# Two-layer diffusion backbone on one core: where the convolution and pooling steps, the prompt's pooling, the first early pairs and two stores stand in the order of work

## The chip, the core and the metric

The kernel runs on one core of one Trainium2 chip. The metric is the device time of one execution in microseconds (us); three runs are shown as their median. The profile is of one execution of its own.

## What is computed

Two layers over 1024 sample tokens and 128 prompt tokens, width 1024, in float32. Cut to what matters:

```python
def trunk_layer(x, cond, ...):
    mod = silu(cond) @ w_mod + b_mod                 # shift, scale, gate
    hn = rms_norm(x, g_pre) * (1 + scale) + shift
    a_b, a_c, a_x, a_z, q_down, kv_down, b_z, c_u, c_z, merge_logits = split(hn @ w_in)
    y_a = silu(a_z) * (a_b * centred_conv3(a_c * a_x, conv_w, conv_b))
    y_b = silu(b_z) * attention(q_down, kv_down, cached latents, rope)
    y_c = silu(c_z) * multiscale_pool(c_u, pool_w, pool_scale)   # windows 2, 4, 8, 16
    gates = sigmoid(merge_logits)
    merged = sum over n of gates[n] * ([y_a, y_b, y_c][n] @ w_branch[n])
    return x + gate * rms_norm(merged @ w_o, g_post)
```

The sample pass and the prompt pass share the weights. `multiscale_pool` takes, for each of four groups of 128 channels, the mean over a window along the tokens, subtracts the input, and multiplies by a 128 by 128 matrix.

## The kernel before

Every float32 operand of a product is split into a high part, rounded for TensorE, and the rest, and a product is three matmuls (high by high, low by high, high by low; `mm3`, line 109). ScalarE or GpSimd makes the high part (`a_copy` line 67, `p_copy` line 82), VectorE the rest (`sub`, line 90). The tokens stand in two chunks of 512 columns. SBUF has 44 slots `S` of 1040 columns and 12 slots `H` of 512, PSUM 8 banks `PS`. Each engine executes its instructions in the order in which the Python program emits them, and so do the DMA queues of SP, ScalarE and GpSimd; so the order of emission is the schedule.

A layer has these stages.

- **Input product** (`in_phase`, line 829). The columns of `w_in` are taken as 29 pairs of 256 columns. Each pair (class `Pair`, line 562) has a generator `prep` (line 567): it asks SP for the raw weights, then makes splits, one piece for each call. Twenty pairs are *full*, in the order of `ORDER` (line 822): 8 to 15, 19 to 22, 16, 17, 18, 23, 24, 26, 27, 28. A full pair (`run`, line 688) makes seven products of 12 matmuls each (a Strassen form over halves of the weights and both chunks) and one product for the prompt. Nine pairs (`EARLY`, line 27) are cut in two: two products of the first chunk and the prompt's product are done *early* (line 656), while the second chunk is still being normalised, and the other five products *late*, after all full pairs. The early stage takes the first three pairs together, in loops over products, and the others singly.
- **What a pair leaves** is stored to DRAM: gates, the convolution's factors (pairs 8 to 15, two for each of four blocks of channels: `d_t` and `d_zb`), the latents (16 to 18), the pooling's inputs and gates (19 to 22, one for each group: `d_u`, `d_z`).
- **Background generators.** `spawn` (line 135) puts a generator on a list, and each `tick` (line 139) calls every one of them once; a full pair makes four ticks, a late one three. `conv_gen` (line 870) does the convolution of the sample tokens, six calls for each of four blocks, and goes on with `s_pool` (line 1017), four groups with windows 2, 4, 8 and 16. A group loads its input, adds shifted copies of it (`window_sum`, line 981: one, two, three or four additions of some 1030 columns, in one call), makes means, splits, multiplies, and stores `d_yc`. It is spawned after pair 15. `p_conv` (line 898) does the prompt's convolution and goes on with the prompt's pooling (`p_pool`, line 1055, 15 calls); it is spawned after pair 28, the last full pair. `mod_bg` (line 339) makes the modulation rows of later use, in layer 0.
- **Stores that wait.** `put` (line 118) emits a store on SP three `step`s later, so that SP doesn't stand before data that is not there yet; `flush` emits all of them at once. A store emitted with `sp.dma_start` directly makes SP wait for its data, and all later loads with it.
- **Merges** (`mid_phase`, line 1214). `merge` (line 932) multiplies a branch by its weights and gates and adds; the first takes the convolution's output, the second the pooling's. Each makes 26 ticks. During the first, `kv_lat` normalises and turns the key latents; during the second run `p_kv` (line 1165, the prompt's latents, with two transposes on TensorE, each three pauses after the row norm that it needs) and `q_lat` (query latents, with a column sum of squares on TensorE, a product with a matrix of ones).
- **Attention** (`produce`, `attention`), the third merge (`last_merge`), and the **output product** (`out_phase`, line 1775): `post_chunk` (line 1711) normalises a chunk, adds the residual and, in layer 0, makes the next layer's input and its early form; `out_prompt` (line 1758) does the same for the prompt. Between the layers, the splits of the first two early pairs of layer 1 are made during the last output group (`ahead`, line 633), and the rest of both chunks' norms is on the background list while the early pairs run.

## Time and profile before

| | us |
|---|---|
| median of 3 runs | 2816.55 |
| lowest and highest | 2812.87 and 2819.08 |
| the profiled execution's own time | 2811.16 |
| its span, first to last instruction | 2809.4 |

The profile is that one execution. A busy TensorE is not TensorE at its peak, and the granted clock of TensorE has two levels, 2.4 GHz (written 1.00) and 1.2 GHz (0.50); the mean over a stretch is given. In the order of time a row is a run of like instructions of one engine, with its start, its length, their count, and in brackets how long the engine had stood idle before it and what ended that. A row of the busy time by stage gives the stretch and its length, then busy time and count of instructions of PE, PEld, DVE, ACT and POOL, then the granted clock, the share of DMA and GB/s.

### The profile page before, as it was taken

What the parts mean: (1) busy time and instruction counts of PE and PEld (TensorE: products, weight loads), DVE (VectorE), ACT (ScalarE), POOL (GpSimd) and SP (SyncE); (2) the same over time, 40 slices, a digit from 0 to 9 for tenths busy, and PEclk for the clock granted to TensorE, in tenths of its full rate; (3) what the DMA queues carried; (4) which work ended last, traced back from release to release, by engine and by line L of the source; (5) the groups of instructions that cost most, each with busy time, mean ns of one, the idle gap of its engine ahead of it and who ended that gap; (6) DMA issues with size and microseconds to landing.
All of it is one profiled execution on the core that took longest, in us unless ns stands there. A gap on an engine that the chain in (4) does not pass through costs nothing. (4 is left out here: it accounts for less than half of the span.)

```text
span 2809.4 us, 32642 instructions
## 1 busy us (share of the span) xinstructions
PE 2578.5 (92%) x11672; PEld 2040.9 (73%) x11672; DVE 1836.5 (65%) x2434; ACT 1024.5 (36%) x1694; POOL 893.1 (32%) x757
## 2 busy tenths in 40 slices
PE   4899999997898889999978999999979988999997
PEld 2777777775676767777757888887857766776786
DVE  5745566676656578886567565766767557888655
ACT  4521122232221357773344222223223124677621
POOL 2222211112122545753022232111222145477502
PEclk7999999998999999999989999999989999999999
DMA  7333245555479300006154222443535871000333
GB/s 280 126 115 108 94 162 178 189 171 168 136 270 323 131 5 8 23 31 201 57 180 155 95 71 83 163 160 130 185 126 191 283 265 27 5 8 31 120 117 113
DMA packets 218403, 371.02 MB, mean 132 GB/s; under 512 B 21120, under 2 KB 106112, under 8 KB 218240
## 3 DMA queue, kind: packets, MB, share of 16 engines
q1 hardware_dynamic: 186560, 308.36, 33.1%
q10 hardware_dynamic: 27072, 43.79, 4.2%
q0 software_dynamic: 4608, 16.78, 1.7%
q8 instruction: 92, 1.51, 0.2%
q14 instruction: 71, 0.58, 0.1%
HBM read 254.45 MB, written 112.23 MB: 131 GB/s over the span
## 5 line engine op out<-in xcount | busy, mean ns | idle before, releaser
L107 PE MATMUL p<-s,s 128*128 128x512 f32 (+3 forms) x10876 | 2459.2, 385 | 132.4 <-ACT s L68 40.7
L107 PEld LDWEIGHTS p<-s,s 128*128 128x128 f32 (+1 forms) x10876 | 1945.2, 190 | 618.4 <-ACT s L68 49.3
L88 DVE TENSOR_TENSOR s<-s,s 128x1024 fp32r<-128x1024 f32 (+7 forms) x565 | 662.3, 1180 | 381.3 <-ACT s L68 155.0
L88 POOL TENSOR_TENSOR s<-s,s 128x512 f32<-128x512 f32 (+2 forms) x109 | 203.7, 1872 | 764.2 <-DMA s<-in_w_in_dram 605.5
L88 DVE TENSOR_TENSOR h<-p,h 128x512 f32<-128x512 f32 (+1 forms) x480 | 315.2, 659 | 197.4 <-PE p L107 125.8
L68 ACT CAST s<-s 128x1024 fp32r<-128x1024 f32 (+4 forms) x283 | 276.9, 988 | 452.1 <-DVE s L88 273.7
L88 DVE TENSOR_TENSOR s<-h,s 128x512 fp32r<-128x512 f32 (+4 forms) x316 | 298.4, 956 | 118.6 <-ACT s L79 60.8
L82 POOL TENSOR_SCALAR s<-s 128x1024 fp32r<-128x1024 f32 (+2 forms) x123 | 149.4, 1217 | 496.4 <-DVE s L88 123.8
L79 ACT ACTIVATE h<-h 128x512 f32<-128x512 f32 (+1 forms) x196 | 123.2, 629 | 470.7 <-DVE h L88 354.4
L79 ACT ACTIVATE h<-p 128x512 f32<-128x512 f32 (+2 forms) x364 | 208.5, 573 | 229.1 <-PE p L107 214.0
L79 ACT ACTIVATE s<-p 128x512 fp32r<-128x512 f32 x288 | 174.1, 604 | 2.4 <-POOL h L88 2.4
L88 DVE TENSOR_TENSOR h<-h,h 128x512 f32<-128x512 f32 (+3 forms) x122 | 89.7, 735 | 119.8 <-ACT h L79 95.2
L88 POOL TENSOR_TENSOR s<-s 128x512 f32<-128x512 f32 x94 | 131.9, 1414 | 77.7 <-DVE s L88 45.1
L1492 DVE TENSOR_REDUCE c<-p 128x1 f32<-128x448 f32 x256 | 147.8, 610 | 5.5 <-PE p L107 5.4
L68 ACT COPY h<-p 128x512 f32<-128x512 f32 (+2 forms) x108 | 51.6, 478 | 235.1 <-PE p L107 219.7
L88 POOL TENSOR_TENSOR h<-h,h 128x512 f32<-128x512 f32 (+2 forms) x72 | 96.3, 1338 | 105.5 <-DVE h L88 68.2
L88 POOL TENSOR_TENSOR s<-h,s 128x512 fp32r<-128x512 f32 x64 | 89.7, 1402 | 115.9 <-ACT s L79 113.3
L88 DVE TENSOR_TENSOR s<-p,s 128x512 f32<-128x512 f32 (+2 forms) x118 | 71.4, 631 | 51.6 <-PE p L107 21.5
L68 ACT CAST s<-h 128x512 fp32r<-128x512 f32 (+5 forms) x92 | 47.8, 524 | 152.8 <-DVE h L88 91.5
L68 ACT COPY s<-p 64x512 f32<-64x512 f32 (+3 forms) x116 | 64.1, 567 | 98.7 <-PE p L107 70.2
L88 POOL TENSOR_TENSOR s<-s,h 128x512 f32<-128x512 f32 x26 | 39.9, 1542 | 116.8 <-DVE h L100 76.3
L103 POOL TENSOR_SCALAR s<-s,cols 128x512 f32<-128x512 f32 x24 | 29.8, 1252 | 97.6 <-ACT s L79 68.3
(116 smaller groups left out, 933.1 us busy)
## 6 DMA issues: line engine op xcount, KB each, us to landing
s<-in_w_in_dram SPq DMA_DIRECT2D x296, 256.0 KB, 4.6
s<-in_w_mod_dram SPq DMA_DIRECT2D x48, 512.0 KB, 5.8
d_gate<-h ACTq DMA_DIRECT2D x96, 256.0 KB, 3.3
s<-d_gate SPq DMA_DIRECT2D x64, 256.0 KB, 5.7
d_part<-s SPq DMA_DIRECT2D x64, 256.0 KB, 2.2
s<-in_w_br_dram SPq DMA_DIRECT2D x24, 512.0 KB, 3.8
s<-in_xT_dram SPq DMA_DIRECT2D x16, 512.0 KB, 7.6
d_ya<-s SPq DMA_DIRECT2D x16, 512.0 KB, 2.6
```

What stands on the lines that cost most here:

```text
L68: act.copy(out=out, in_=in_)
L79: act.activation(out=out, in_=in_, func=func, scale=scale, bias=bias)
L82: pool.tensor_scalar(out=out, in0=in_, scalar1=1.0, scalar2=0.0, op0=ALU.mult, op1=ALU.add)
L88: eng.tensor_tensor(out=out, in0=in0, in1=in1, op=op)
L103: (eng or dve).tensor_scalar(out=out, in0=in0, scalar1=s1, scalar2=s2, op0=op0, op1=op1)
L107: pe.matmul(out=out, lhsT=lhsT, rhs=rhs, start=start, stop=stop)
L1492: dve.reduce_max(out=mv[:, i, qt:qt + 1], in_=ps[:, 0:448], axis=AX.X)
```

## The change

- `conv_gen` is spawned after pair 8. A list `done` holds the number of the last full pair that is through (never going down until the next layer's pair 8). Block m of the convolution waits until pair 9 + 2m is through, group gi of the pooling until pair 19 + gi; until then a call does nothing.
- `window_sum` becomes the generator `window_gen`, which pauses after each addition; `s_pool` passes the pauses on, `pooled` (the prompt) doesn't.
- `p_pool` is no longer the end of `p_conv`; it is spawned at the start of `mid_phase`, with its output slot, and has to be finished when the first merge is.
- In `early`, the first three pairs are made ready one by one, each just before its first product, and no longer all three before the first.
- In `p_kv` each of the two groups of three pauses becomes seven.
- The stores of `d_x` use `put`; the store of `d_xp` goes to GpSimd's queue. `post_chunk` pauses after its loads for the second chunk too.
- In `out_phase` of layer 0 the calls of `post_chunk` and `out_prompt` that followed the last prompt product are put into a generator `first`, which the early stage of layer 1 calls once, after the first early product.

```diff
@@ early
             first, steps = len(us) > 1, 2 if us[0] in units[-2:] else 1
+            p1 = []
             for u in us:
                 ready(u)
-            p1 = []
-            for u in us:
                 h = H()
                 a_copy(h, u.prod(u.w[0], 0, "11"))
@@ in_phase
             run(l, x, epis[x.p], None if last else u[i + 1], hooks)
-            if x.p == 15:
+            if x.kind == "full":
+                done[0] = max(x.p, done[0])
+            if x.p == 8:
+                done[0] = 8
                 g1 = spawn(conv_gen(l))
-            elif x.p == 24:
-                g1_done = g1
             if x.p == 28:
-                ypc.append(S(F32R))
-                g2 = spawn(p_conv(l, yp, ypc[0]))
+                g2 = spawn(p_conv(l, yp))
         finish(g2)
-        return ya, yp, ypc[0]
+        return ya, yp
@@ conv_gen
-        flush()
         for m in range(4):
+            while done[0] < 9 + 2 * m:
+                yield
+            flush()
             t, v = S(), S()
...
-        flush()
         yield from s_pool(l)
@@ p_conv
-        yield from p_pool(l, ypc)
@@ window_sum, now window_gen
             d = o
-        return d, tiles[(gi + 1) % 2]
+            yield
+        got += [d, tiles[(gi + 1) % 2]]
@@ s_pool
         for gi in range(4):
+            while done[0] < 19 + gi:
+                yield
+            flush()
             u = S()
...
-            d, o = window_sum(u, gi, 1024, [S(), S()])
-            yield
-            means(d, o, u, gi, 1024)
+            got = []
+            yield from window_gen(u, gi, 1024, [S(), S()], got)
+            o = got[1]
+            means(got[0], o, u, gi, 1024)
             yield
@@ p_kv, in both places
-            yield
-            yield
-            yield
+            for _ in range(7):
+                yield
@@ mid_phase
-        yc = []
+        yc, ypc = [], S(F32R)
+        gp = spawn(p_pool(l, ypc))
...
-        finish(R["first"])
+        finish(R["first"], gp)
@@ post_chunk
         xs = load_x(l, c)
-        if not quick:
-            yield
+        yield
...
-            sp.dma_start(out=d_x[c, kp], in_=outs[i][:, 0:1024])
+            put(d_x[c, kp], outs[i][:, 0:1024])
@@ out_prompt
-            sp.dma_start(out=d_xp, in_=out[:, 0:1024])
+            pool.dma_start(out=d_xp, in_=out[:, 0:1024])
@@ out_phase
-        gB = spawn(post_chunk(l, 1, B, True))
+        gB = post_chunk(l, 1, B, True)
+        next(gB)
+        gP = out_prompt(l, xp, gps, out, cs)
         if l + 1 < L:
-            prompt(0, lambda: next(gB, None))
-        else:
-            prompt(1, lambda: adv(gB, 2))
-            next(gB)
             prompt(0)
-        if l + 1 < L:
-            next(gB)
-        gP = out_prompt(l, xp, gps, out, cs)
+
+            def first():
+                for g in (gB, gB, gP, gB, gP, gB):
+                    next(g)
+                spawn(gB), spawn(gP)
+                yield
+
+            return (gP, gB), units, first()
+        prompt(1, lambda: adv(gB, 2))
+        next(gB)
+        prompt(0)
         next(gP, None)
         next(gB, None)
-        if l + 1 < L:
-            next(gP)
-            next(gB)
-        spawn(gP)
-        return (gP, gB), units if l + 1 < L else None
+        return (gP, gB), None, None
@@ the loop over layers
-            R = mid_phase(l, *in_phase(l, units, None if l else mid(), pend))
+            R = mid_phase(l, *in_phase(l, units, then if l else mid(), pend))
...
-            pend, units = out_phase(l, mg, pt)
+            pend, units, then = out_phase(l, mg, pt)
```

## Rows read from the trace of the kernel before

**Rows 1.** The page: busy time of TensorE, and its slices.
```profile
PE 2578.5 (92%) x11672; PEld 2040.9 (73%) x11672; DVE 1836.5 (65%) x2434; ACT 1024.5 (36%) x1694; POOL 893.1 (32%) x757
...
PE   4899999997898889999978999999979988999997
```

**Rows 2.** Busy time by stage: full and late pairs, layer 0, then layer 1.
```profile
397.00:640.00 243.00, 241.27 (x1154) 187.38 (x1153) 155.72 (x188) 65.36 (x89) 37.59 (x36) 1.00 0.50 168
640.00:818.00 178.00, 150.35 (x629) 116.22 (x627) 123.49 (x192) 41.66 (x68) 41.35 (x45) 0.91 0.54 181
...
1741.00:2012.40 271.40, 266.82 (x1286) 220.92 (x1285) 184.86 (x206) 74.96 (x101) 47.04 (x42) 1.00 0.44 149
2012.40:2176.10 163.70, 143.74 (x589) 113.77 (x587) 113.69 (x179) 41.27 (x67) 42.32 (x45) 0.93 0.52 171
```

**Rows 3.** Order of time, late pairs of layer 0.
```profile
673.36 7.65 DVE L88 TENSOR_TENSOR s<-s 128x1039 f32<-128x1039 f32 x4
...
681.67 0.69 PE L908 MATMUL p<-ident,s 128*128 128x128 f32 x2 [6.73 <-DVE h L88]
...
689.60 8.50 PE L107 MATMUL p<-s,s 128*128 128x512 f32 x24 [7.24 <-DVE h L100]
...
728.86 1.30 POOL L88 TENSOR_TENSOR s<-s,s 128x512 f32<-128x512 f32 x1 [24.66 <-DMA s<-in_w_in_dram]
...
743.31 1.87 PE L107 MATMUL p<-sel,h 128*128 128x2 f32 x8 [11.22 <-ACT h L68]
```

**Rows 4.** Order of time, late pairs of layer 1.
```profile
2042.32 6.85 DVE L88 TENSOR_TENSOR s<-s 128x1039 f32<-128x1039 f32 x4
...
2049.92 4.90 PE L107 MATMUL p<-s,s 128*128 128x512 f32 x12 [6.38 <-DVE h L88]
...
2075.73 14.05 PE L107 MATMUL p<-s,s 128*128 128x512 f32 x60
...
2105.91 14.20 PE L107 MATMUL p<-s,s 128*128 128x512 f32 x48 [4.58 <-DVE h L88]
```

**Rows 5.** VectorE by line and shape, 397 to 640 us: busy, mean ns, idle before.
```profile
L88 DVE TENSOR_TENSOR s<-s,s 128x1024 fp32r<-128x1024 f32 x44 | 55.3, 1257 | 36.6 <-ACT s L68 26.2 <-PE p L107 10.2
...
L88 DVE TENSOR_TENSOR s<-s 128x1039 f32<-128x1039 f32 x3 | 3.7, 1234 | 0.0
```

**Rows 6.** Order of time, start of the second merge of layer 0.
```profile
885.35 4.48 SPq L1130 DMA_DIRECT2D s<-d_kvq  x6
...
892.87 0.90 PE L1182 MATMUL p<-ident,h 128*128 128x128 f32 x3 [8.18 <-DVE h L103]
...
894.45 2.58 DVE L88 TENSOR_TENSOR s<-s,s 128x1024 f32<-128x1024 f32 x2 [1.63 <-ACT s L79]
...
899.28 1.88 PE L107 MATMUL p<-s,ones 128*128 128x512 f32 x4
```

**Rows 7.** Order of time, the prompt's pooling in layer 0: two calls.
```profile
777.10 0.98 DVE L88 TENSOR_TENSOR s<-s 128x143 f32<-128x143 f32 x3
...
779.48 0.29 DVE L88 TENSOR_TENSOR s<-s,s 128x128 fp32r<-128x128 f32 x1 [0.41 <-ACT s L68]
...
789.98 1.31 DVE L88 TENSOR_TENSOR s<-s 128x143 f32<-128x143 f32 x4
...
792.65 0.29 DVE L88 TENSOR_TENSOR s<-s,s 128x128 fp32r<-128x128 f32 x1 [0.36 <-ACT s L68]
```

**Rows 8.** Order of time, between the layers.
```profile
1438.95 1.45 PE L107 MATMUL p<-h,ones 128*128 128x512 f32 x2 [4.02 <-DVE h L88]
...
1457.25 0.44 ACT L79 ACTIVATE c<-c 128x1 f32<-128x1 f32 x2 [1.36 <-POOL c L103]
...
1460.73 0.80 PE L107 MATMUL p<-s,s 128*128 128x512 f32 x1 [12.84 <-ACT s L68]
...
1480.00 1.48 PE L107 MATMUL p<-h,ones 128*128 128x512 f32 x2 [3.37 <-DVE h L88]
```

**Rows 9.** Order of time, the first early pairs of layer 0.
```profile
60.56 1.22 PE L107 MATMUL p<-s,s 128*128 128x512 f32 x2 [10.77 <-ACT s L79]
```

More of the change, by code (lines that the diff above doesn't have):

```diff
@@ L837, in in_phase @@
         flush()
-        ya, yp, ypc = [], S(F32R), []
+        ya, yp = [], S(F32R)
         def load_ya(m):
@@ L894, in conv_gen, with p_conv @@
             yield
-        flush()
         yield from s_pool(l)
-    def p_conv(l, yp, ypc):
+    def p_conv(l, yp):
         tz = S()
@@ L979, in merge, with window_gen @@
         flush()
-    def window_sum(u, gi, n, tiles):
+    def window_gen(u, gi, n, tiles, got):
         w = n + 16
@@ L985, in window_sum @@
         s = 1
-        for step in range(gi + 1):
-            o = tiles[step % 2]
-            if step == 0:
+        for step_ in range(gi + 1):
+            o = tiles[step_ % 2]
+            if step_ == 0:
                 lo += 1
@@ L995, in window_sum @@
             d = o
-        return d, tiles[(gi + 1) % 2]
+            yield
+        got += [d, tiles[(gi + 1) % 2]]
     def pooled(u, gi, n, tiles):
-        d, o = window_sum(u, gi, n, tiles)
-        means(d, o, u, gi, n)
-        return o
+        got = []
+        for _ in window_gen(u, gi, n, tiles, got):
+            pass
+        means(got[0], got[1], u, gi, n)
+        return got[1]
     def means(d, o, u, gi, n):
@@ L1015, in hybrid_step_kernel @@
     PW = {}
+    done = [0]
     def s_pool(l):
@@ L1030, in s_pool @@
                 split(pw[0], pw[1], raw)
-            d, o = window_sum(u, gi, 1024, [S(), S()])
-            yield
-            means(d, o, u, gi, 1024)
+            got = []
+            yield from window_gen(u, gi, 1024, [S(), S()], got)
+            o = got[1]
+            means(got[0], o, u, gi, 1024)
             yield
@@ L1195, in p_kv @@
             ts(eq[:, 0:384], eq[:, 0:384], r, 0.0)
-            yield
-            yield
-            yield
+            for _ in range(7):
+                yield
             pt = PS()
@@ L1212, in kvq_post, with mid_phase @@
         return R
-    def mid_phase(l, ya, ypa, ypc):
+    def mid_phase(l, ya, ypa):
         lead[0] = 4
@@ L1713, in post_chunk @@
         xs = load_x(l, c)
-        if not quick:
-            yield
+        yield
         r = rstd(bsum(O_["acc"]), DM)
@@ L1805, in out_phase @@
         finish(gA)
-        gB = spawn(post_chunk(l, 1, B, True))
+        gB = post_chunk(l, 1, B, True)
+        next(gB)
+        gP = out_prompt(l, xp, gps, out, cs)
         if l + 1 < L:
-            prompt(0, lambda: next(gB, None))
-        else:
-            prompt(1, lambda: adv(gB, 2))
-            next(gB)
             prompt(0)
-        if l + 1 < L:
-            next(gB)
-        gP = out_prompt(l, xp, gps, out, cs)
+            def first():
+                for g in (gB, gB, gP, gB, gP, gB):
+                    next(g)
+                spawn(gB), spawn(gP)
+                yield
+            return (gP, gB), units, first()
+        prompt(1, lambda: adv(gB, 2))
+        next(gB)
+        prompt(0)
         next(gP, None)
         next(gB, None)
-        if l + 1 < L:
-            next(gP)
-            next(gB)
-        spawn(gP)
-        return (gP, gB), units if l + 1 < L else None
+        return (gP, gB), None, None
     with tc.manual_schedule():
```

## The prediction

> **What bounds the kernel now.** The page comes first: TensorE is busy for 92% of the span, no other engine comes near, and the slices say where the rest is [rows 1]. The first two of the forty slices, 10 and 11, 13 to 15, 21 and 22, 30, 33 and 34, and the last are below nine tenths; elsewhere TensorE hardly stops. So a change can earn only what TensorE loses in its own holes, and what the halved clock after a hole costs. The table by stage sizes them [rows 2]. The last nine ("late") pairs of layer 0 take 178 us, of which TensorE is busy for 150.35; those of layer 1 take 163.7 us with 143.74. A late pair is five products, 60 matmuls, and 60 matmuls take 14.05 us when nothing is in the way [rows 4], so nine need 126.5 us. The stretches before them, full pairs with the convolution and three of the four pooling groups in the background, lose 1.73 us in 243 and 4.58 us in 271.4 [rows 2]. The background work fits among full pairs (84 matmuls and a prompt product each) and not among late ones.
>
> The order of time shows the mechanism [rows 3]. At 673.36 VectorE does the four window sums of the last pooling group in one piece, 7.65 us; TensorE waits 6.73 us for what VectorE does next, and 7.24 us more behind the rest of that group. Then the loads come late: GpSimd has waited 24.66 us for raw weights at 728.86, and TensorE stands 11.22 us until 743.31 behind the split of those weights. Layer 1 does the same at 2042.32: four sums in 6.85 us, then a wait of 6.38 us, and 4.58 us before 2105.91 [rows 4].
>
> **The parts of the change and their prices.**
>
> *Pooling out of the late pairs.* The convolution generator starts after pair 8, not after pair 15, and follows its pairs, so it ends with the first full pairs that come after 15. A group of the large pooling then takes 7 calls and one per window sum: 8, 9, 10, 11, together 38. A full pair makes four ticks, and twelve full pairs follow pair 15: 48 ticks, less some six for the last convolution block. So all four groups are over before the first late pair. The late pairs keep the prompt's convolution; the prompt's pooling leaves. What goes: in layer 0 27.65 us of idle time [rows 2] and the slow clock. Its granted mean of 0.91 means 32 us at 1.2 GHz; if about as much of that is idle as is work it costs 6 to 8 us, and one stretch of it, 24 matmuls in 8.50 us [rows 3] against 5.6 at the pace of [rows 4], cost 2.9. I take 6: 33.6. In layer 1 19.96 us of idle time [rows 2], and 2.1 and 3.0 us seen at the slow clock (12 matmuls in 4.90 us, 48 in 14.20) [rows 4]; with the shorter ones 6: 26. The matmuls of pooling only move. Nothing in TensorE's order forces a rest, but late pairs give VectorE little slack, so I leave 3 us standing in each layer: **-30.6 and -23**. Bounds: -34 to -15 and -26 to -12 (half of it stays, because the convolution of the prompt and the single load queue were part of the cause).
>
> *The fourth group among full pairs.* Three groups and the convolution cost 1.73 and 4.58 us there [rows 2]; a fourth costs a third of that: **+2** for both layers. Bounds 0 and +8 (the same waits once more, doubled).
>
> *The prompt's query and key sums ask for their transposes four ticks later.* At the start of the second merge TensorE waits 8.18 us for the prompt's normalised key rows [rows 6]. Four more pauses take the wait away from that place. But TensorE's next stop is 18 matmuls further: the column sum of the query latents, whose squares land one by one and whose second addition on VectorE ends at 894.45 + 2.58 = 897.03, while TensorE reaches that sum now at 899.28 [rows 6]. It would reach it about 8 us earlier and wait there. What is won is 2.25 us a layer, **-4.5**, not 16. Bounds: -21 (both waits and some 2 us of slow clock each go, if the loads land earlier too) and 0.
>
> *Prompt pooling in the first merge.* Its 15 ticks fit in that merge's 26, and TensorE's part is small. VectorE's part is not free: in this merge's second quarter it runs behind TensorE through the key norm, and the chain that ends in the late loads of [rows 6] starts there. The two heavy calls, eight and sixteen wide, last 777.10 to about 779.8 and 789.98 to 792.94 [rows 7], 2.7 and 2.9 us. Both stand in VectorE's queue before the merge's next four evacuations; behind those stand the partial stores on SP, the rope loads, and the next merge's fetches. Bounds per layer: 0 (its queue has waits to absorb them) and +5.6 (all of it is passed on). I take the middle, as the rope steps behind it do wait for loads: **+5.6** for both layers.
>
> *The seam between the layers.* Now TensorE waits 4.02 us for the square sum of the second chunk, and 12.84 us before the third early pair's first product, which is behind that pair's split on ScalarE [rows 8]. After the change the first early product stands before that sum and fills the first wait. It doesn't shorten the chain: the calls that normalise the prompt stand in ScalarE's queue, in the order they had, ahead of the third pair's split, and their last functions run at 1457.25 [rows 8]. So TensorE has done the second pair sooner and then waits longer: it resumes some 1.5 us earlier. Behind it, the third pair's weights are asked for without standing behind the prompt's store, which is on GpSimd's queue now, and the fourth pair's not behind the four chunk stores, which are put off by three steps. VectorE's fold then doesn't stand behind a split that waits for its load, and the wait of 3.37 us at 1480.00 [rows 8] goes: **-5**. Bounds -20.2 (all three waits) and +3 (the later request of the third pair is late itself). The prompt's store costs nothing in its new place, where GpSimd waits for ScalarE anyway.
>
> *The first early pairs of layer 0.* Here the three loads are already asked for, and asking singly only moves splits: the second pair's split now stands behind the first product's copy and the first modulation rows. The large hole, 10.77 us before 60.56 [rows 9], hangs on the second chunk's norm and keeps its order, with a subtraction of the third pair's split (1.26 us, [rows 5]) put ahead: **+2**, bounds -1 and +5.
>
> The last output stage has the same calls in the same order but for four loads, and the large stages between are not touched: 0.
>
> **Sum.** -30.6 - 23 + 2 - 4.5 + 5.6 - 5 + 2 = -53.5. The profiled execution took 2811.16 us (span 2809.4), so 2757.6; the median of the runs shown, 2816.55, lies 5.4 us above it, which gives 2763.
>
> **Rivals.**
> 1. *The second merge gives all back.* If the loads of the query latents land some 8 us earlier, and prompt pooling hides, 16 us and the slow clock go besides: 2763 - 16.5 - 5.6 = 2741. For it: the load queue is freed in other places. Against it: those loads are issued at 885.35, after the first merge's last stores [rows 6], which the change doesn't move.
> 2. *The full pairs pay.* VectorE's window sums last 1.23 us among full pairs [rows 5], but 7.65 / 4 = 1.91 us where GpSimd's weight sums run beside them [rows 3]. With the convolution among pairs whose products GpSimd multiplies, and all pooling in single steps between its sums, some 40 wide steps a layer at 0.68 us more are 27 us of VectorE time; if half reaches TensorE, 13.5 a layer, the time is 2790. Against it: the groups already there show 1.23. The Trainium skill has this as a rule: SBUF — State Buffer, section "Who interferes with whom", says that a VectorE instruction with two SBUF inputs contends with a GpSimd instruction that reads SBUF. By that rule the sums would slow wherever both run; the late stretch agrees with its 1.91, the full stretch with its 1.23 does not show it.
> 3. *Slower.* The pooling's loads and stores stand in SP's single queue ahead of the raw weights. Where one group met the late pairs, it cost 6.73 + 7.24 = 14 us [rows 3]. If each of the eight groups, now stretched over more ticks, does that among full pairs, 112 us are paid: 2875. It turns the sign from 53.5 / 8 = 6.7 us a group on. Against it: three groups a layer pass there for at most 4.58 us.
> 4. *It moves nothing.* If the late pairs starve by their own loads and the prompt's convolution, their holes stay, and the small terms cancel: 2816. Against it: the last late pairs of layer 1 run 60 matmuls in 14.05 us [rows 4].
>
> **The numbers.** Forecast 0.62, rival 1 0.12, rival 2 0.15, rival 3 0.06, rival 4 0.05. About 0.2%, 5.6 us, is what a measurement of this kernel tells from no change. Faster are the forecast and the first two rivals, 0.89; same 0.05; slower 0.06. The range takes in rivals 1 and 2 and the bounds of the two late terms: 2737 to 2796.
>
> **What would show it.** In the changed profile the windows of the late pairs should be some 130 to 150 us long with TensorE busy nearly throughout, no 128x1039 sum in them, and the raw weights no longer 24 us late. The wait before the transposes at the second merge should be gone and one of 6 to 9 us stand before the four matmuls against the ones, about 18 matmuls earlier or later. At the seam one hole of about 16 us should replace two. I am wrong if late pairs still show waits of 6 us, if full pairs lose over 7 us a group, or if the second merge starts with no wait at all.

## The result, and where the time went in the profile after

The changed kernel takes 2832.11 us (median of 7 runs, 2823.87 to 2835.96), the kernel before 2814.21 in the runs beside it: a ratio of 1.0056, 95% interval 1.0041 to 1.0071. It is slower by 0.6%, where the prediction had 2763 us and faster. The profiled execution took 2832.24 us with a span of 2830.5, that is 21.1 us more than the span before.

The page answers to [rows 1]: TensorE's busy time grew by 15.1 us though it executes as many matmuls as before, and the page's first lines no longer show where.

```profile
PE 2593.6 (92%) x11672; PEld 2050.3 (72%) x11672; DVE 1831.6 (65%) x2434; ACT 1022.9 (36%) x1694; POOL 907.2 (32%) x758
...
PE   5799999999997989989978999999999988999997
```

So both traces were cut at the same events: in the order of time, the start of each full pair's product for the prompt (its first 128x256 matmul) and that of the attention's first; for the merges, VectorE's first product with a gate, and the eighteenth, where the second merge begins; for the end of the attention, one of its last 128x256 products (the 61st `p<-h,s` of the layer). The lengths of the stretches, in us:

| stretch | before | after | difference | forecast |
|---|---|---|---|---|
| start to the first full pair's prompt product | 155.1 | 162.3 | +7.2 | +2 |
| layer 0, first eight intervals of the full pairs | 192.5 | 209.4 | +16.9 | 0 |
| layer 0, the later ones | 275.2 | 282.5 | +7.3 | +1 |
| layer 0, late pairs up to the first gate product | 197.6 | 167.9 | -29.7 | -30.6 |
| layer 0, first merge | 56.5 | 69.4 | +12.9 | +2.8 |
| layer 0, second merge | 65.5 | 67.5 | +2.0 | -2.25 |
| attention | 292.0 | 295.0 | +3.0 | 0 |
| third merge, output product, seam and early pairs of layer 1 | 328.0 | 325.0 | -3.0 | -5 |
| layer 1, first eight intervals | 178.5 | 198.8 | +20.3 | 0 |
| layer 1, the later ones | 254.6 | 263.4 | +8.8 | +1 |
| layer 1, late pairs | 187.8 | 147.7 | -40.1 | -23 |
| layer 1, first merge | 59.3 | 69.0 | +9.7 | +2.8 |
| layer 1, second merge | 64.9 | 68.1 | +3.2 | -2.25 |
| the rest | 501.9 | 504.2 | +2.3 | 0 |

What the change was to bring came: the late pairs won 69.8 us, more than the 53.6 forecast. It was given back, and more, in stretches where the forecast had nearly nothing. The busy time by stage of the kernel before shows the full pairs, the first eight intervals and the later ones, layer 0 and then layer 1, and behind them the late pairs of both layers (columns as in [rows 2]):

```profile
155.10:347.60 192.50, 192.50 (x922) 152.70 (x921) 102.91 (x126) 38.26 (x51) 51.98 (x40) 1.00 0.30 96
347.60:622.80 275.20, 273.47 (x1306) 212.82 (x1305) 172.99 (x205) 71.82 (x98) 41.70 (x39) 1.00 0.53 176
1562.40:1740.90 178.50, 178.50 (x866) 148.97 (x864) 98.05 (x112) 37.21 (x49) 51.98 (x40) 1.00 0.21 69
1740.90:1995.50 254.60, 250.02 (x1201) 206.83 (x1200) 171.06 (x188) 69.47 (x93) 43.39 (x39) 1.00 0.46 154
...
622.80:820.40 197.60, 168.22 (x718) 130.28 (x717) 136.17 (x210) 47.62 (x77) 45.24 (x48) 0.92 0.53 177
1995.50:2183.30 187.80, 162.83 (x678) 129.18 (x677) 128.73 (x198) 47.80 (x76) 45.99 (x48) 0.93 0.51 171
```

The same six stretches after the change:

```profile
162.30:371.70 209.40, 199.02 (x921) 156.37 (x921) 119.51 (x141) 41.30 (x54) 55.51 (x40) 0.97 0.37 120
371.70:654.30 282.60, 278.34 (x1318) 216.22 (x1317) 169.38 (x212) 73.14 (x101) 43.69 (x41) 0.99 0.48 156
1579.20:1778.00 198.80, 185.68 (x866) 152.84 (x865) 116.43 (x127) 40.28 (x52) 54.44 (x39) 0.96 0.28 94
1778.00:2041.40 263.40, 254.40 (x1213) 209.53 (x1212) 171.12 (x197) 71.70 (x98) 44.60 (x41) 0.99 0.39 132
...
654.30:822.20 167.90, 159.85 (x686) 124.26 (x685) 107.43 (x145) 39.68 (x63) 46.53 (x46) 0.97 0.58 194
...
2041.40:2189.20 147.80, 147.74 (x652) 119.57 (x652) 100.10 (x132) 39.26 (x61) 47.11 (x46) 1.00 0.60 198
```

The first eight intervals before are without a hole: in layer 1, 178.50 us busy in 178.50. After the change the same 866 matmuls are spread over 198.80 us: 13.1 us of holes, and 7.2 us more for the matmuls themselves, whose granted clock was 0.96 in the mean and not 1.00. All of it stands in three of the eight intervals, which take 30.2, 28.2 and 29.0 us instead of 22.3. VectorE is busy for 18 us more, with three of the four blocks of the convolution. In the later intervals 12 matmuls and some 2.5 to 4.4 us of holes came in. The late pairs of layer 1 are full: 147.74 in 147.80; the waits of [rows 4] are gone.

Where a hole of the first eight intervals comes from is read backwards in the order of time, layer 1, after the change:

```profile
1642.00 5.12 SPq L125 DMA_DIRECT2D d_t<-h  x2
1642.56 1.28 DVE L100 SCALAR_TENSOR_TENSOR s<-s,vec,s 128x1023 f32<-128x1023 f32 x1
...
1643.76 0.69 DVE L88 TENSOR_TENSOR h<-p,h 128x512 f32<-128x512 f32 x1
1644.36 1.28 DVE L100 SCALAR_TENSOR_TENSOR s<-s,vec,s 128x1023 f32<-128x1023 f32 x1
1644.52 2.25 POOL L88 TENSOR_TENSOR h<-h,h 128x512 f32<-128x512 f32 x1 [2.55 <-DVE h L88]
...
1647.21 2.52 SPq L576 DMA_DIRECT2D s<-in_w_in_dram  x4
...
1654.08 1.31 POOL L88 TENSOR_TENSOR s<-s,s 128x512 f32<-128x512 f32 x1 [7.30 <-DMA s<-in_w_in_dram]
...
1655.42 4.48 DVE L88 TENSOR_TENSOR s<-s,s 128x512 f32<-128x512 f32 x3 [5.79 <-POOL s L88]
...
1668.86 0.63 ACT L79 ACTIVATE h<-h 128x512 f32<-128x512 f32 x1 [4.41 <-DVE h L88]
1669.40 1.03 ACT L68 CAST s<-s 128x1024 fp32r<-128x1024 f32 x1
...
1670.48 0.79 PE L107 MATMUL p<-s,s 128*128 128x512 f32 x1 [4.83 <-ACT s L68]
```

TensorE waits for ScalarE's split of the next weights (1669.40), which stands behind an activation that waited 4.41 us for a sum of VectorE. VectorE is late since it had waited 5.79 us for GpSimd's sum of raw weights, and GpSimd 7.30 us for the weights themselves. SP asked for them only at 1647.21, behind the two stores of `d_t`, which waited for GpSimd's product at 1644.52; and that product had waited for VectorE's 0.69 us sum, which stood between two steps of the convolution. The chain runs through all five engines. Whether SP's queue is a link of it, or VectorE's work alone does it, is what the first experiments ask.

In the first merge of layer 0 and at the start of the second the order of time shows two waits that weren't there before, in the first and the last of these rows:

```profile
860.10 0.90 PE L107 MATMUL p<-s,h 128*128 128x128 f32 x3 [5.01 <-ACT s L68]
860.81 41.72 PE L107 MATMUL p<-s,s 128*128 128x512 f32 x168
912.26 3.78 PE L107 MATMUL p<-s,ones 128*128 128x512 f32 x4 [9.73 <-DVE s L88]
```

The first wait is the prompt's pooling itself: the last three of its small products wait for ScalarE's split, and all of TensorE's work with them. The other takes the place of the wait before the transposes of [rows 6], as forecast. At the seam one hole has taken the place of the first two of [rows 8], and the wait near 100 us has grown from 8.07 us to 13.34:

```profile
115.93 0.80 PE L107 MATMUL p<-s,s 128*128 128x512 f32 x1 [13.34 <-ACT s L68]
...
1477.43 0.79 PE L107 MATMUL p<-s,s 128*128 128x512 f32 x1 [16.53 <-ACT s L68]
...
1527.96 0.80 PE L107 MATMUL p<-s,s 128*128 128x512 f32 x1 [7.10 <-ACT s L68]
```

### The profile page after: what moved, and what is told of

The parts are those of the page before. It is cut to its first block, busy times and chain, and to the rows that moved or that the text cites. A ratio compares the mean times of both kernels' runs of the same rounds, so it can differ in the third digit from the quotient of the medians.

```text
span 2830.5 us, 32609 instructions
## 1 busy us (share of the span) xinstructions
PE 2593.6 (92%) x11672; PEld 2050.3 (72%) x11672; DVE 1831.6 (65%) x2434; ACT 1022.9 (36%) x1694; POOL 907.2 (32%) x758
## 5 line engine op out<-in xcount | busy, mean ns | idle before, releaser
L88 DVE TENSOR_TENSOR s<-s,s 128x1024 fp32r<-128x1024 f32 (+6 forms) x565 | 658.9, 1174 | 397.4 <-ACT s L68 147.8
L68 ACT CAST s<-s 128x1024 fp32r<-128x1024 f32 (+3 forms) x283 | 276.1, 988 | 465.0 <-DVE s L88 288.3
L88 POOL TENSOR_TENSOR h<-h,h 128x512 f32<-128x512 f32 (+2 forms) x72 | 102.0, 1417 | 132.9 <-DVE h L88 81.0
L107 PE MATMUL p<-s,h 128*128 128x512 f32 (+1 forms) x184 | 55.1, 412 | 12.8 <-ACT s L68 12.7
```

Of the source, the lines that this page charges most:

```text
L68: act.copy(out=out, in_=in_)
L88: eng.tensor_tensor(out=out, in0=in0, in1=in1, op=op)
L107: pe.matmul(out=out, lhsT=lhsT, rhs=rhs, start=start, stop=stop)
```

## The experiments

"After" is the changed kernel; a ratio is to the kernel before in the same comparison, with its 95% interval. Stretches are named and cut as in the table above, each from one profiled execution. Where no edit touches a stretch, its length differs between these profiles by up to 3 us in the first eight intervals, 4 in the merges, 5 in the later intervals, 6 in the late pairs and 12 in the attention. The ratios of four runs (the convolution's stores later, the prompt's pooling back, the early pairs together in both layers, three pauses in the kernel after) overlap with that of the changed kernel, 1.0041 to 1.0071, so there only the stretches tell something.

**The convolution back behind pair 15.**

```diff
-            while done[0] < 9 + 2 * m:
+            while done[0] < 15:
```

> The changed kernel with one edit: all four blocks of the convolution wait for pair 15; the pooling's gates and single steps stay. The first eight intervals between prompt products of the full pairs took 192.5 and 178.5 us before and 209.4 and 198.8 us after, the later ones 7.4 and 8.8 us more after than before. Theory A (the convolution beside its own pairs is what costs there): those eight intervals go back to 192.5 and 178.5 within 3 us, 37 us in all; the pooling then does not end before the late pairs, and 14 of its 38 steps return to them at 5 to 10 us a layer; the time is 2805 to 2815 us. Theory B (the single pooling steps are what costs, the convolution's place does not matter): the later intervals keep or raise their loss, the eight intervals gain under 10 us in all, and the time stays at 2825 to 2845 us.

2812.06 us, ratio 0.9992 (0.9982 to 1.0002). The eight intervals are 192.4 and 178.2 us, as before the change, and the later ones 275.4 and 254.5. The late pairs took back 11.5 and 20.7 us of what they had won (179.4 and 168.4), the first merge 4.8 and 3.0. Theory A holds: the convolution beside its own pairs costs 37 us. With the pooling that follows it the full pairs lost 53 us after the change, and what this made room for had earned 40 (32.2 in the late pairs, 7.8 in the merges).

**The convolution's stores later.** `put_y` is a second list with nine steps.

```diff
-            put(d_ya[0, m], f(hi[:, 0:n]))
-            put(d_ya[1, m], f(lo[:, 0:n]))
+            put_y(d_ya[0, m], f(hi[:, 0:n]))
+            put_y(d_ya[1, m], f(lo[:, 0:n]))
```

> The changed kernel with one edit: the stores of the convolution's result stand nine steps behind their split on SP's queue instead of three, on a list of their own; all else is emitted in the same order. After the change SP waited up to 14 us for ScalarE's split ahead of these stores, with the raw weights of the next pair behind. Theory A (these stores hold the load queue up, and the raw weights are late by that): the waits of 2.8 to 5.3 us before products of the full pairs beside the convolution vanish and the time is 2800 to 2812 us. Theory B (the convolution's own work on VectorE and ScalarE and its slots of memory cost the time, wherever its stores stand): the waits stay and the time is 2827 to 2838 us.

2833.31 us, ratio 1.0075 (1.0051 to 1.0100): nothing won, intervals of 208.6 and 199.2. What SP waited for in the first eight intervals of layer 1, after the change (total, times, longest):

```profile
SPq L125 <- POOL h L88: 72.9, 16, 13.1
SPq L125 <- ACT s L68: 39.1, 3, 14.0
```

and with these stores later:

```profile
SPq L128 <- POOL h L88: 117.9, 16, 20.5
```

(Line 128 there is line 125 here.) The wait for ScalarE's split is gone, and SP stands 45.0 us longer before GpSimd's products. These stores were not the link.

**The factors' stores on GpSimd's queue.** In `keep_prod`:

```diff
             mul(x, x, y, eng=pool)
-            put(dst[c], x)
+            pool.dma_start(out=dst[c], in_=x)
```

> The changed kernel with one edit: the stores of the convolution's factors (d_t and d_zb) go to the queue of GpSimd, which makes those products, at once; on SP's queue they stood ahead of the raw weights and waited 72.9 us in all for GpSimd in the first eight intervals of layer 1. Theory A (SP's queue couples the two: VectorE's convolution steps make the products late, the store behind them holds the raw weights, the next sums come late): the waits before products in the first eight intervals vanish, these take 192 to 197 and 178 to 184 us instead of 209.4 and 198.8, and the time is 2795 to 2806 us. Theory B (VectorE has too much to do there, and the split of the pair's last weights stands behind it on ScalarE): the intervals stay at 205 to 210 and 195 to 200, and the time is 2826 to 2836 us.

2795.31 us, ratio 0.9928 (0.9914 to 0.9943). The eight intervals are 192.7 and 179.1 us, with the convolution still in them. TensorE in layer 1, order of time, is one unbroken run:

```profile
1557.82 184.42 PE L107 MATMUL p<-s,s 128*128 128x512 f32 x896 [0.45 <-DVE s L88]
```

GpSimd's wait for raw weights in that stretch, after the change:

```profile
POOL s L88 <- DMA s<-in_w_in_dram: 49.1, 7, 7.9
```

and with the stores moved:

```profile
POOL s L88 <- DMA s<-in_w_in_dram: 8.2, 2, 7.1
```

Theory A holds: SP's queue is the link. VectorE's steps are not fewer, and the wait is gone. The order of time on SP shows it directly: in layer 1 a pair's request for raw weights stood 19.4 to 21.5 us behind the start of its prompt product in the kernel before, up to 28.3 us behind it after the change, and 13.9 to 16.1 us behind it with the stores moved. The edit also drops `put`'s three steps, so the stores' `H` slots may come free sooner; that part was not tested by itself.

**The convolution's work cut down.**

```diff
-            stt(v[:, 1:n], t[:, 0:n - 1], ...)
...
-            stt(v[:, 0:n - 1], t[:, 1:n], ...)
...
-            mul(v[:, 0:n], v[:, 0:n], z[:, 0:n])
+            mul(v[:, 0:16], v[:, 0:16], z[:, 0:16])
```

> The changed kernel with the sample convolution cut down: both shifted additions are left out and the product with its gate covers 16 columns only, so VectorE has 3.7 us less of wide steps in each block, of some 6.8; loads, slots, stores and ScalarE's part stay. Theory A (what VectorE does for the convolution between two pairs' sums makes the waits): the first eight intervals fall from 209.4 and 198.8 us to under 200 and 188, and the time is 2800 to 2815 us. Theory B (the loads and stores on SP's queue, or the slots of memory that the blocks hold, make them): the waits before products stay at 2.8 to 5.3 us each, the intervals stay within 4 us, and the time is 2822 to 2834 us.

2808.43 us, ratio 0.9971 (0.9956 to 0.9986); intervals of 199.7 and 185.7 us. With half of VectorE's part away, 9.7 and 13.1 us of 16.9 and 20.3 go. So VectorE's steps start the delay and SP's queue carries it on: half of the first gives back more than half of the loss, the other nearly all of it.

**The same stores moved in the kernel before.** The edit of `keep_prod`, alone.

> The kernel before with one edit: the stores of the convolution's factors go to GpSimd's queue at once. In the kernel before, no convolution steps stand beside these pairs, but SP waited 123.7 us in all for GpSimd ahead of stores in the first stretch of layer 1. Theory A (the stores hold the raw weights only where VectorE's convolution steps make the products late): nothing to be won, the first eight intervals stay at 192.5 and 178.5 us and the time is 2808 to 2819 us. Theory B (the store's place is worth its gain by itself, whatever the change does): the eight intervals or the stretch behind them shorten by 10 us or more in all and the time is 2785 to 2805 us.

2814.59 us, ratio 1.0006 (0.9994 to 1.0019); 192.5 and 178.5 us. By itself the place of these stores is worth nothing. SP's waits for GpSimd cost nothing there, 123.7 us of them; what the changed kernel adds beside these pairs is the convolution's work on VectorE.

**The convolution from pair 13, window sums in one call.**

```diff
-            while done[0] < 9 + 2 * m:
+            while done[0] < max(13, 9 + 2 * m):
...
-            yield from window_gen(u, gi, 1024, [S(), S()], got)
+            for _ in window_gen(u, gi, 1024, [S(), S()], got):
+                pass
             o = got[1]
+            yield
```

> The changed kernel with two edits: the convolution starts after pair 13 instead of 9, so that some six of its 24 calls stand beside pairs with GpSimd's products, and the window sums of the sample's pooling are one call for a group again, so that the pooling ends before the late pairs. Theory A (each block beside its own pairs costs its share, and what the late pairs won does not depend on it): the first eight intervals are at most 6 us above those of before (192.5 and 178.5), the late stretch stays at 168 and 148 us as after the change, and the time is 2790 to 2803 us. Theory B (the fourth pooling group only moves its cost from the late to the full pairs): the later twelve intervals grow by 10 us or more over before (275.2 and 254.6), and the time is 2806 to 2820 us.

2813.28 us, ratio 1.0000 (0.9986 to 1.0015). The eight intervals are 6.9 and 5.4 us above those of before, the later ones only 1.9 and 5.0; but the late pairs took back 7.4 and 9.4 (175.3 and 157.1), against theory A. Theory B's time came without its cause. The last group's window sums end just before the late pairs, and its later steps stand among them: what is started later seems to be paid there. The profiled execution took 2824.91 us, 11.6 above the median, so these stretches are less sure than the others.

**The prompt's pooling back among the late pairs.** `p_conv` ends with `yield from p_pool(l, ypc)` again, and the `spawn` in `mid_phase` goes.

> The changed kernel with one edit: the prompt's pooling follows the prompt's convolution again, among the late pairs. The two first merges were 15 us longer each after the change than before. Theory A (the prompt's pooling pushes VectorE's work of that merge back, and the loads behind it): the second merge's start comes some 12 us earlier in both layers, at 20 us or less returned among the late pairs, and the time is 2808 to 2820 us. Theory B (the longer pauses ahead of the prompt's transposes make that loss): the merges stay as they are after the change, the late pairs lose 3 to 8 us each, and the time is 2838 to 2848 us.

2829.52 us, ratio 1.0053 (1.0035 to 1.0071). The first merges fall to 57.7 and 58.6 us, as before the change, and the late pairs rise to 175.2 and 165.4, by 7.3 and 17.7. The merges behave as theory A has it, but more returns than its 20 us: 22.1 us won stand against 25.0 returned, so the time misses both ranges. In the late pairs or in the merge, the prompt's pooling costs about the same. (The 15 us of the expectation are both merges of layer 0 together; the first alone is 12.9 and 9.7 us longer.)

**The first early pairs together again, in both layers.**

```diff
+            for u in us:
+                ready(u)
             p1 = []
             for u in us:
-                ready(u)
                 h = H()
```

> The changed kernel with one edit: the first three early pairs are made ready together again, before the first product. The start up to the first full pair's prompt product took 155.1 us before and 162.3 us after. Theory A (the single requests cost it, since the second pair's split stands behind the first product's copy): 5 to 7 us come back in layer 0; between the layers, where TensorE had 4.02 and 12.84 us of waits before and one of 16.53 after, 3 us or less go either way; the time is 2823 to 2829 us. Theory B (the 13.34 us wait at 102.6 us belongs to what the early stage asks for later, not to the first three): less than 2 us come back and the time is 2830 to 2834 us.

2834.87 us, ratio 1.0075 (1.0056 to 1.0094). The first full prompt product starts at 154.6 us, 7.7 earlier; the stretch with the seam and the early pairs of layer 1 took 330.2 us instead of 325.0. Layer 0 wants the three together, layer 1 singly. The total misses both ranges: theory A has the start right, but not layer 1.

**Together in layer 0 only**, on top of the moved stores:

```diff
+            for u in us if first and us[0].l == 0 else ():
+                ready(u)
             for u in us:
                 ready(u)
```

> The kernel with the factors' stores on GpSimd's queue (2795.3 us), with one more edit: in layer 0 the first three early pairs are made ready together, as before the change; in layer 1 singly, as after it. Theory A (the single requests cost layer 0 some 7 us at its start and win a little between the layers): the first full pair's prompt product starts at 155 to 156 us instead of 163.1, the rest stays, and the time is 2785 to 2791 us. Theory B (what is won at the start is waited for again behind it): 2793 to 2798 us.

2783.99 us, ratio 0.9902 (0.9882 to 0.9921): start at 154.9, the stretch with the seam and the early pairs 325.0. Theory A, a little better than its range.

**Prompt pooling in single steps**, with the moved stores. `pooled` gives way to `yield from window_gen(...)` and `means`.

> The kernel with the factors' stores on GpSimd's queue (2795.3 us), with one more edit: the prompt's pooling pauses after each window addition, so that its 15 calls become 25 and no call puts more than one addition, or the means and the split, on VectorE at once. The first merge took 72.8 and 68.4 us, against 56.5 and 59.3 before. Theory A (the heavy calls stand in one piece ahead of the merge's products on VectorE): the first merge falls by 5 us or more in each layer and the time is 2780 to 2789 us. Theory B (the amount of VectorE's work in this merge counts, not its grouping, and the calls reach further into the merge): the first merge stays within 3 us or grows, and the time is 2792 to 2803 us.

2792.22 us, ratio 0.9932 (0.9915 to 0.9948). The first merges are 69.5 and 63.9 instead of 72.8 and 68.4 us, but the stop before the small products grew to 10.11 us, and the second merge of layer 0 is 2.4 us longer. The merges lie between the theories, the time at the edge of theory B's range: cutting into pieces is at most a part of it.

**The small products later**, on top of the kernel of 2784.0 us:

```diff
-            yield
-            yield
+            for _ in range(6):
+                yield
             pw = PW[l]
```

> The kernel of 2784.0 us with one more edit: the prompt's pooling pauses six times, not twice, ahead of each of its two groups of six small products in the first merge. In that merge TensorE stood 4.98 us in each layer before the last three of these products, which wait for ScalarE's split behind VectorE; the merge took 73.0 and 68.3 us (56.5 and 59.3 before the change). Theory A (the products stand too early in TensorE's order, and this stop with the slow clock behind it is a good part of what the merge lost): the stop goes, the first merge falls by 6 us or more in each layer, and the time is 2766 to 2775 us. Theory B (VectorE's added work holds back what the merge's own sums and loads need, and the stop only stands where that shows): a stop of 4 us or more stands elsewhere in the first or at the start of the second merge, both merges together shorten by 3 us or less a layer, and the time is 2779 to 2788 us.

2776.19 us, ratio 0.9878 (0.9855 to 0.9901). The order of time in the first merge of layer 0, to the start of the second:

```profile
853.00 0.78 PE L107 MATMUL p<-s,h 128*128 128x128 f32 x6
853.61 23.82 PE L107 MATMUL p<-s,s 128*128 128x512 f32 x102
889.60 3.78 PE L107 MATMUL p<-s,ones 128*128 128x512 f32 x4 [12.17 <-DVE s L88]
```

The stop is gone: six small products in one run. The first merges fall by 6.0 and 7.9 us, to 67.0 and 60.4. The wait before the ones grew from 8.39 us to 12.17, and the second merges by 2.7 and 1.4, so 3.3 and 6.5 us are left. The outcome lies between the theories: the stop cost something of its own, and part of it was only the place where VectorE's delay shows. This is the fastest kernel of the study, 1.2% below the kernel before; its ratio's interval overlaps that of the kernel of 2784.0 us, so the total alone does not show this last step.

**Three pauses again ahead of the prompt's transposes**, in the kernel after.

```diff
# in both places
-            for _ in range(7):
+            for _ in range(3):
```

> The changed kernel with one edit: the prompt's query and key sums pause three times again ahead of their transposes, not seven times. From the first to the second merge's end marker the second merge took 65.5 and 64.9 us before and 67.5 and 68.1 us after the change. Theory A (the wait of 8.18 us only moves to the column sum, as the prediction has it, and the longer pauses bring at most 2 us a layer): the wait of 8 us stands before the transposes again, and the second merge is 0 to 3 us longer or shorter than 67.8; the time is 2829 to 2837 us. Theory B (the longer pauses push the query latents' work back and are what made the second merge longer): the second merge falls to 65 us or less in both layers, the time to 2826 to 2828 us.

2837.18 us, ratio 1.0072 (1.0048 to 1.0095). The second merges are 65.7 and 64.4 us, 1.8 and 3.7 shorter, and the wait stands before the transposes (9.20 us). Theory A, just outside both its ranges: the place of the wait changes and the second merges shrink a little, while the attention of layer 0, at 299.9 us instead of 295.0, takes more than that back. **The same edit on the kernel of 2784.0 us:**

> The kernel of 2784.0 us with one more edit: three pauses again ahead of the prompt's transposes. Theory A (the longer pauses lengthen the second merge, and the single call for the window sums was what made the kernel of 2797.3 us slower): the second merges fall from 67.1 and 66.7 to 65.5 and 64.5 us, the later twelve intervals stay at 284.6 and 260.9, and the time is 2779 to 2784 us. Theory B (the longer pauses help elsewhere, in the attention that follows): the second merges fall likewise, the stretch from the first attention to the first full pair grows by 5 us or more, and the time is 2786 to 2797 us.

2791.25 us, ratio 0.9922 (0.9895 to 0.9949). Second merges of 66.3 and 64.9 us; the attention of layer 0 took 294.2 us against 290.0. The pattern is theory B's, but the ratio's interval overlaps that of 2784.0, and the attention, whose code no edit touches, took anything from 287.5 to 299.9 us in these profiles. With three pauses it was longer than in the kernel with seven that the run starts from, each time (by 4.8 us above and 4.2 here, and by 9.5 in the run below, which has a second edit); but the kernel before, with three, took 292.0 us against 295.0 after the change. So it is open whether the pauses help there.

**Both the pauses and the one-call window sums**, on the same kernel.

> The fastest kernel so far (factors' stores on GpSimd's queue, first early pairs together in layer 0; 2784.0 us), with two more edits in separate stretches: the window sums of a group of the sample's pooling in one call again, and three pauses again ahead of the prompt's transposes. In that kernel the later twelve intervals take 284.6 and 260.9 us (275.2 and 254.6 before), the second merges 67.1 and 66.7 (65.5 and 64.9). Theory A (single window additions between the pairs' sums cost the full pairs what the fourth group seems to cost, and the longer pauses lengthen the second merge): the later intervals fall to 278 and 257 or less, the second merges to 65.7 and 64.5, and the time is 2768 to 2777 us. Theory B (a fourth group and the convolution cost the same there however they are cut, and the second merge's wait only moves): the later intervals stay within 3 us, and the time is 2781 to 2788 us.

2797.26 us, ratio 0.9943 (0.9925 to 0.9961). The second merges fell (65.3 and 64.5), the later intervals rose to 287.1 and 266.8. Single steps in the sample's pooling are the better form, if anything, and the fourth group's cost does not come from them.

## Why the prediction was wrong

**The step that failed** is *the fourth group among full pairs: +2*, and within it the convolution, which the forecast moved beside its own pairs without a price. It argued from the stretches of [rows 2], where the convolution and three groups cost 1.73 and 4.58 us, that the same work would cost nothing a few pairs earlier. But the pairs of those stretches leave no products to GpSimd. Beside pairs 8 to 15 a pair's own product waits for VectorE, its store for the product, and the next raw weights for the store. Measured: +37.2 us in the first eight intervals, of which the moved stores give back 36.4, and +53.3 among the full pairs in all. The later intervals add 16.1 us, of which 12 matmuls a layer, 2.8 us in each by the pace of [rows 4], only moved there from the late pairs; what the other 10.5 us wait for was not taken apart.

**Rival 3 had the place and the wrong carrier.** It put stores in SP's queue ahead of the raw weights and asked 6.7 us a group; the stores that held the queue were the convolution's factors, which the change does not touch, made late by steps that it moved. Its chance of 0.06 was judged by pooling groups that pass among pairs without such stores.

**Rival 2 falls as the cause.** With the stores moved, the convolution's 128x1023 steps still take 1280 ns each, as after the change, and the cost is gone. Its price did not come either: of the twenty window sums of the changed kernel nineteen take 1.22 to 1.24 us and one 2.07. The 1.23 us that the prediction held against the rule of this rival were no test of it: during all twelve window sums among the full pairs of the kernel before, GpSimd stood idle.

**The late pairs** were mis-sized to the other side: -29.7 in layer 0 (forecast -30.6) but -40.1 in layer 1 (forecast -23). Layer 0's agreement is partly luck: 8.05 us of holes stay, where 3 were left standing, and TensorE's own time fell by 8.4 us for 32 matmuls fewer, where the slow clock had been put at 6. In layer 1 the holes went whole, 24.97 us and not the 19.96 that [rows 2] shows: its window ends 7.2 us before the first gate product, and three waits for loads of `d_ya`, 5.0 us, lie in between. TensorE's own time fell by 15.1 us there. Without the prompt's pooling leaving as well both layers would have won 22.4 and 22.3, by the run that brings it back; the forecast gave its departure no price of its own.

**Prompt pooling in the first merge** was mis-sized: forecast +5.6 for both layers, with 5.6 a layer as the bound; measured +12.9 and +9.7. VectorE's added work was in the sum, TensorE's stop before the small products was not; moving these won 3.3 and 6.5 us in the kernel of 2784.0. What keeps layer 0's first merge at 67.0 us there, against 56.5 before, was not taken apart.

**The pauses** were right on the wait and wrong on what follows it. The wait went from the transposes to the ones, as forecast, 9.73 us where 6 to 9 were expected, and it stays at 9.75 with the prompt's pooling out of the first merge. Counted from the start of the second merge, the column sum starts after 20.6 us instead of 22.4 in layer 0, and 19.3 instead of 21.9 in layer 1: 1.8 and 2.5 us won, about the 2.25 forecast. But from that sum to the attention's first product it is 3.8 and 5.7 us longer, which the forecast put at nothing. From the sum on, in layer 0, before and after:

```profile
899.28:918.80 19.52, 19.11 (x80) 14.29 (x78) 15.31 (x28) 4.36 (x9) 2.98 (x3) 1.00 0.82 296
...
912.26:933.90 21.64, 21.64 (x79) 15.82 (x79) 13.50 (x27) 3.75 (x8) 4.58 (x4) 0.87 0.89 307
```

The slow clock that followed the wait before the transposes (granted 0.69 between 892.87 and 899.28 us, ahead of the sum) now falls on the sum and what comes after it, 2.1 us, and TensorE's next wait for VectorE grew from 1.35 to 2.61 us. So the second merges are 2.0 and 3.2 us longer, not 2.25 shorter, and three pauses take 0.8 to 3.7 us off them.

**The seam** came as described, one hole of 16.5 us for two, and the wait of 3.37 us is gone; but it is worth 3.0 us of the 5 forecast. All of that is won up to the end of the hole, where the forecast had 1.5. From there to the first full pair's prompt product the two kernels take 101.7 and 101.8 us, since the wait before the fourth pair's first product grew from 2.27 to 7.10 us; what that one hangs on was not followed. **The first early pairs** cost 7.2 to 8.3 us against a bound of 5: the wait before 60.56 us of [rows 9] was looked at, and fell to 4.74 us; the one that grew, by 5.3 us, stands some 50 us further on, at 115.93.

## What to carry to other kernels

Work that was free in one stretch need not be free in the next: before moving a step, list for the new place what waits for the engine it runs on, and follow that chain through the stores to the load queue. Where a shared queue also carries the next loads, try the store of what an engine has just made on that engine's own queue; here the move changed nothing before the change, and decided the sign after it. A wait on a queue is no loss by itself: 123.7 us of them cost nothing in the kernel before. The small products of a background task stopped TensorE for 5 us in each layer, so such products should be emitted some ticks after their operands are due. And where a wait is moved, the slow clock behind it moves as well and has to be priced at its new place.

## What the runs showed of the hardware

A store on GpSimd's queue holds GpSimd for 0.59 us, with the stores moved, in the first eight intervals of layer 1:

```profile
L784 POOL DMA_DIRECT2D d_t<-h x8 | 4.7, 589 | 2.4 <-POOL h L88 2.4
```

It lands in 3.9 us (`d_t`) and 2.4 us (`d_zb`), medians of 16 stores each. From SP's queue in the kernel before, the trace has the landing of three of the 32 stores alone (2.0, 3.4 and 2.7 us), so whether the store itself is slower is not shown. Moving these stores won 36.8 us. The Trainium skill, DMA: Bandwidth & Descriptors, section "SWDGE vs HWDGE vs iDMA", advises SP or ScalarE as the issuer of a plain transfer, as the faster to set up; by it these stores would have stayed on SP's queue. The time went the other way, since what counted was what stood behind the store in the queue.

VectorE's 128x512 subtractions of the raw weights' sums took, in the first eight intervals of layer 1 after the change,

```profile
L88 DVE TENSOR_TENSOR s<-s,s 128x512 f32<-128x512 f32 x16 | 18.6, 1162 | 23.2 <-POOL s L88 22.9
```

and with the stores moved

```profile
L88 DVE TENSOR_TENSOR s<-s,s 128x512 f32<-128x512 f32 x16 | 11.6, 724 | 0.3
```

In the first case seven of the sixteen begin while GpSimd is in its second sum and take 1.76 to 1.78 us each, the other nine 0.68 to 0.69; in the second case only one meets GpSimd, and takes 1.28. The rule of rival 2 (the Trainium skill, SBUF — State Buffer, section "Who interferes with whom") agrees with that; but the kernel before has the same 1162 ns in the mean and no hole, so this slowing alone makes none. Whether its 7.0 us of VectorE time add to the holes after the change was not tested. Attention stretches of the same code differed by up to 12 us between profiles; why was not found.
